# The first stage of a two-block transformer kernel rebuilt: own load buffers, sums and a bias table on TensorE, partial sums kept in banks

## The chip, the cores and the metric

The kernel runs on one core of one Trainium2 chip, with fp32 inputs and outputs for one sequence of 256 tokens. The metric is the device time of one execution in microseconds. Several runs are timed, and their median is what a prediction speaks of; one further execution was profiled.

## The reference

Two layers of a first block, then one layer of a second block, over x of 256 x 2048. Cut to what the change touches:

```
c_act = silu(c)
for l in range(2):
    mod = c_act @ w_mod[l] + b_mod[l]              # 2048 x 6144
    shift, scale, gate = split(mod, 3)
    h = rmsnorm(x, norm_gain[l]) * (1 + scale) + shift
    proj = h @ w_in[l]                             # q, k, v, gates, index heads
    ...
    bias = rel_bias[t5_bucket(pos[query] - pos[key])]   # 32 buckets, 8 heads
    logits = q @ k * scale + bias                  # sparse attention on the top 64 keys
    ...                                            # rotary, retention, group norm
    x = x + gate * (y @ w_out[l])
# second block: gated convolution, recurrence, a gate from the rmsnorm, final rmsnorm
```

t5_bucket gives a distance below 16 a bucket of its own and puts larger ones into 16 logarithmic buckets; distances of 128 and more share the last.

## The kernel before

Every product of the projections is made in three matmuls of split numbers. A weight chunk of 256 rows and up to 512 columns is loaded on SP's queue as `raw`; ACT rounds it to `whi` (L236), DVE subtracts to get `wlo` (L238), three buffers each. TensorE then does 12 matmuls per chunk (L254 hi by hi, L255 lo by hi, L256 hi by lo; two halves of the sequence, two row blocks), into two banks of the four that the tag `mm` has.

The input projection of layer 0 has ten column groups (nine of 512 columns, one of 336). Its rows of `w_in` are taken in four quarters, because the rows of h in quarter q need the modulation of just those 512 features. In each quarter all ten groups get two chunks, so 20 chunks or 240 matmuls a quarter. What a group has gathered is copied by ACT to a tile `sp` or `gate` in the first quarter (L931) and added there by DVE in the others (L934).

The modulation of a quarter (`mod_quarter`) loads 16 blocks of 512 KB (`graw`, in the first quarter `raw` too), which DVE multiplies by a scalar of c and adds up (L355, L357). Eight matmuls with one column each (L365) sum over partitions; L367 to L370 make shift `Sh` and gain `Gm`, and L560/L563 the rows of h from the transposed and normalised x. `first_rows` does all this as a background job. Its first part is the first stage: x is loaded on ACT's queue, vectors on POOL's (`vecs`, L304 and L312, transposed on TensorE in L315 and L316 and copied to `vT` by DVE), ACT squares x (L504), DVE reduces to `tot` (L534), POOL makes the reciprocal root in six small steps (`rstd`, L156 to L165), DVE makes two diagonal matrices `dg` (L540), and 32 matmuls (L203) transpose and scale x, which ACT copies back (L545).

The bias table is a background job from the second quarter on (`rel_rotary`, then `bias_table`): distances are computed on POOL and DVE and written to memory as bytes (`reld`), read back broadcast to 32 buckets by 4 rows (`rb`), turned to ones and zeros by three ACT passes (L483, L484, L486) in 24 blocks of 512, looked up with two matmuls a block (L469), copied (L471) and stored (`biasd`). Selection waits for it in the fourth quarter (`until("select")`).

A list scheduler with priorities (`tc.high_priority`, `AHEAD`) settles the order on each engine when the program is built; `spawn` gives a background job a rate at which its steps are mixed into the main work. Each engine then takes its instructions strictly in that order.

## Time and profile before

| what | us |
|---|---|
| median of three runs | 1931.42 (1928.2 to 1932.54) |
| the profiled execution, its own time | 1935.11 |
| its span, first to last instruction | 1933.3 |
| busy: PE, DVE, ACT, POOL | 1841.2, 1310.0, 1041.2, 109.0 |
| first main matmul starts at | 43.91 |
| the four quarters of layer 0's first projection end at | 101.39, 169.67, 236.19, 307.03 |

The ends of the quarters are read from the timeline of the main matmuls, 80 of L254 in each quarter. Since the program of each engine is a fixed queue, a stretch is best read by what TensorE does in it and what it waits for; the other engines' idle time matters only where TensorE waits for them.

### The profile page before, as it was taken

To read this page: it belongs to the slowest core of one execution; us is meant where nothing else is said; L and a number is where in the kernel's file an instruction comes from. 1 tells how busy PE (TensorE), PEld (TensorE's weight loads), DVE (VectorE), ACT (ScalarE), POOL (GpSimd) and SP (SyncE) were. 2 spreads that over 40 slices of the span, in tenths; PEclk is the share of its full clock that TensorE was granted. 3 is DMA by queue.
4 is the path that set the end of the run, shared out by engine and by line. 5 is a ranking of instruction groups with operands and counts; after the bars stand their busy time and mean duration, and the time that the engine had idled before them with its cause. 6 is when DMAs were issued, how large, how long until landed. Compare 5 with 4: busy or idle time off the path is not lost.

```text
span 1933.3 us, 24130 instructions
## 1 busy us (share of the span) xinstructions
PE 1841.2 (95%) x8670; PEld 1500.1 (78%) x8670; DVE 1310.0 (68%) x1705; ACT 1041.2 (54%) x1576; POOL 109.0 (6%) x220
## 2 busy tenths in 40 slices
PE   3989999998989999999999999999999999999997
PEld 3867677777867787788778778878887888888886
DVE  6788889988667779966655656656665545555564
ACT  3567674645445546356455764466545444445554
POOL 2000040002010005000110000000000000000100
PEclk9999999999989999999999999999999999999998
DMA  9988888887888999865557665556556666656664
GB/s 315 319 289 290 274 296 259 289 290 237 295 281 269 314 301 312 274 202 157 161 184 219 205 186 163 155 161 197 164 151 191 194 191 193 195 185 218 186 202 146
DMA packets 230921, 440.37 MB, mean 228 GB/s; under 512 B 19728, under 2 KB 32144, under 8 KB 230672
## 3 DMA queue, kind: packets, MB, share of 16 engines
q1 hardware_dynamic: 228880, 436.38, 71.3%
q10 hardware_dynamic: 1440, 2.34, 0.4%
q8 instruction: 68, 1.11, 0.2%
q14 instruction: 53, 0.43, 0.1%
q0 software_dynamic: 480, 0.10, 0.0%
HBM read 430.85 MB, written 7.91 MB: 227 GB/s over the span
## 4 chain that ended last, share of the span: by engine, by line
PE 64%; DMA 14%; DVE 10%; ACT 5%; issue 5%; POOL 2%; SPq 1%; ACTq 0%; DVEq 0%; POOLq 0%
PE mm L255 19%; PE mm L256 19%; PE mm L254 19%; DMA graw<-in_w_mod_dram 6%; DVE wlo L238 4%; DVE acc L357 2%; DMA rb<-reld 2%; DMA raw<-in_w_in_dram 2%; ACT whi L236 2%; PE tr L201 2%; DMA raw<-in_w_out_dram 1%; PE tr L1153 1%; DMA dec<-in_k_dec_dram 1%; DMA L<-biasd 1%; DMA raw<-in_w_mod_dram 1%
## 5 line engine op out<-in xcount | busy, mean ns | idle before, releaser
L238 DVE TENSOR_TENSOR wlo<-raw,whi 128x1024 fp32r<-128x1024 f32 (+1 forms) x596 | 721.0, 1212 | 408.8 <-ACT whi L236 407.0
L236 ACT CAST whi<-raw 128x1024 fp32r<-128x1024 f32 (+1 forms) x596 | 620.9, 1044 | 676.0 <-PE mm L256 437.2
L255 PE MATMUL mm<-wlo,ah 128*128 128x512 f32 (+1 forms) x2368 | 933.6, 394 | 14.1 <-DVE wlo L238 13.8
L254 PE MATMUL mm<-whi,ah 128*128 128x512 f32 (+1 forms) x2368 | 933.8, 397 | 13.7 <-ACT ah L192 7.8
L256 PE MATMUL mm<-whi,al 128*128 128x512 f32 (+1 forms) x2368 | 931.0, 393 | 0.5 <-DVE al L193 0.3
L255 PEld LDWEIGHTS mm<-wlo,ah 128*128 128x128 f32 x2368 | 447.5, 189 | 119.8 <-DVE wlo L238 32.6
L254 PEld LDWEIGHTS mm<-whi,ah 128*128 128x128 f32 x2368 | 446.4, 189 | 109.7 <-ACT whi L236 10.4
L256 PEld LDWEIGHTS mm<-whi,al 128*128 128x128 f32 x2368 | 447.1, 189 | 93.0 <-DVE al L193 2.4
L357 DVE SCALAR_TENSOR_TENSOR acc<-graw,ct,acc 128x1024 f32<-128x1024 f32 x174 | 222.7, 1280 | 51.5 <-DMA graw<-in_w_mod_dram 50.9
L934 DVE TENSOR_TENSOR sp<-sp,mm 128x512 f32<-128x512 f32 (+1 forms) x64 | 41.8, 657 | 8.4 <-PE mm L256 8.2
L201 PE MATMUL tr<-blob,ev 128*128 128x128 f32 x192 | 35.8, 277 | 11.5 <-DVE ev L1181 3.8
L184 ACT ACTIVATE ev<-tr,vT 128x128 f32<-128x128 f32 x112 | 32.4, 375 | 17.1 <-PE tr L201 17.1
L201 PEld LDWEIGHTS tr<-blob,ev 128*128 128x128 f32 x192 | 24.1, 141 | 21.2 <-issue 8.4
L156 POOL TENSOR_SCALAR rv<-tot 128x1 f32<-128x1 f32 (+1 forms) x9 | 2.8, 307 | 660.2 <-DVE tot L208 646.8
L504 ACT ACTIVATE junk<-xs 128x512 bf16<-128x512 f32 (+1 forms) x42 | 25.6, 610 | 22.1 <-DMA xs<-in_x_dram 10.0
L158 POOL TENSOR_TENSOR ry<-rv,mhalf 128x4 f32<-128x4 f32 (+2 forms) x33 | 31.8, 965 | 2.7
L201 PE MATMUL tr<-blob,xs 128*128 128x128 f32 x128 | 24.2, 281 | 5.3 <-ACT xs L995 3.6
L1153 PEld LDWEIGHTS tr<-X 128*128 128x128 f32 x224 | 27.0, 192 | 2.0 <-ACT uT L1203 1.0
L483 ACT ACTIVATE oh<-rb,blob 128x512 f32<-128x512 uint8 x24 | 16.4, 717 | 22.5 <-DMA rb<-reld 22.5
L1153 PE MATMUL tr<-X 128*128 128x128 f32 x224 | 27.5, 276 | 0.1
L156 POOL TENSOR_SCALAR rv<-ssq 128x4 f32<-128x4 f32 x12 | 4.5, 371 | 402.4 <-ACT junk L504 402.2
L156 POOL TENSOR_SCALAR rv<-var 128x4 f32<-128x4 f32 x8 | 5.2, 645 | 361.5 <-DVE var L853 361.3
(275 smaller groups left out, 1227.3 us busy)
## 6 DMA issues: line engine op xcount, KB each, us to landing
raw<-in_w_in_dram SPq DMA_DIRECT2D x416, 512.0 KB
graw<-in_w_mod_dram SPq DMA_DIRECT2D x186, 512.0 KB
raw<-in_w_out_dram SPq DMA_DIRECT2D x64, 512.0 KB
raw<-in_w_o_dram SPq DMA_DIRECT2D x32, 512.0 KB
raw<-in_w_ple_gate_dram SPq DMA_DIRECT2D x32, 512.0 KB
raw<-in_w_a_out_dram SPq DMA_DIRECT2D x16, 512.0 KB
raw<-in_w_b_out_dram SPq DMA_DIRECT2D x16, 512.0 KB
raw<-in_w_in_dram SPq DMA_DIRECT2D x16, 256.0 KB
```

Source lines behind the costliest of these rows:

```text
L158: G.tensor_tensor(y, v, mhalf[:, 0:n], op=OP.pow)
L184: A.activation(e[:, s], ps[:, s], AF.Copy, scale=gain[:, i:i + 1])
L201: T.transpose(ps[:, s], src[:, s], ident)
L236: A.copy(hi, raw)
L238: V.tensor_sub(lo, raw, hi.bitcast(F32))
L254: T.matmul(o, ah, hi[:, j, :], start=first, stop=False)
L255: T.matmul(o, ah, lo[:, j, :], start=False, stop=False)
L256: T.matmul(o, al, hi[:, j, :], start=False, stop=end)
L357: last[0] = V.scalar_tensor_tensor(acc, rf, ct[:, j:j + 1], acc, op0=OP.mult, op1=OP.add)
L504: A.activation(junk[:, :n], src, AF.Square, accum_out=acc)
L934: V.tensor_add(h, h, pt[:, :n])
L1153: T.matmul(ps[:, h * P:(h + 1) * P], X[:, h, s], X[:, h, s], start=True, stop=True)
```

## The change

**First quarter's modulation and rows.** They are written out in a function `first_quarter` that is called ahead of the layer. The first 13 of its 16 modulation blocks go to 256-KB tiles of their own (26 tiles `sw` in the tags `ah` and `al`); DVE sums them 512 wide. The last three blocks (`PEJ`) go to `graw` and are not added on DVE: TensorE sums them with the columns of `ct` as vector, 24 more matmuls of one column. The vector loads go from POOL's queue to ACT's; four of the eight x loads go to SP's. The copies to `vT`, the diagonals `dg` and half the copies of transposed x change between DVE and ACT.

**The bias table.** Positions, `rel_bias`, a constant `k_half` and the rows of distances are loaded on POOL's queue at the very start. Rows of distances (bf16, six tiles `rb` in the tags `whi` and `wlo`) are broadcast by a matmul with a selection matrix (L494), compared with the edges by one Sign activation (L496), looked up with two matmuls (L503), four blocks to a bank and one copy (L506). 11 of the 24 broadcasts use the `mm` banks. The table's 24 stores are the background job of the second quarter (`store_table`); the rest of its making, with the rotary tables, is in the first stage and the first quarter.

**Partial sums.** In the second and third quarter ACT copies a group's sums into its two banks before the group (L257), the matmuls add to them, and ACT copies the sums out (L999). Only the fourth quarter adds on DVE.

```diff
-AHEAD = {"wdma": 20, "whi": 30, "wlo": 35, "gdma": 0, "gdve": -10, "tail": -5}
-WJ, NB = 12, 6
+AHEAD = {"wdma": 20, "whi": 30, "wlo": 35, "gdma": 0, "gdve": -10, "tail": -5, "sums": 10}
 RAW, GRAW, WB, EV = 3, 3, 3, 5
+PEJ, EARLY = 3, 11
...
-        def wgroup(srcs, n, aT, kts, consumer, mode="k", tw=3):
+        def wgroup(srcs, n, aT, kts, consumer, mode="k", tw=3, sums=None):
 
             pts = [mmt(), mmt()]
+            if sums:
+                with tc.high_priority(offset=AHEAD["sums"]):
+                    for t in (0, 1):
+                        A.copy(pts[t][:, :n], sums[t][:, :n])
...
-                    first = ci == 0 and j == 0
+                    first = ci == 0 and j == 0 and not sums
...
-                G.dma_start(v1[r:r + n // P, 0:P], v[c0:c0 + n].rearrange("(r c) -> r c", c=P))
+                A.dma_start(v1[r:r + n // P, 0:P], v[c0:c0 + n].rearrange("(r c) -> r c", c=P))
...
-            V.tensor_copy(vT, ps[:, 0:P])
-            V.tensor_copy(vT2, ps[:, P:P + 64])
+            A.copy(vT, ps[:, 0:P])
+            A.copy(vT2, ps[:, P:P + 64])
...
+            rows = []
+            for n in range(6):
+                t, r0 = (0, 16 * n) if n < 2 else (1, 8 * n - 16)
+                rows.append(wp.tile([P, 2048], BF, name="rb", tag="wlo" if n % 2 else "whi", bufs=WB))
+                G.dma_start(rows[n][0:4], bass.AP(tensor=reld[t].tensor, offset=reld[t].offset + r0 * (t + 1) * P,
+                                                  ap=[[32 * (t + 1) * P, 4], [1, 2048]]))
+            for n in range(6):
+                t, r0 = (0, 16 * n) if n < 2 else (1, 8 * n - 16)
+                blocks = []
+                for i in range(4):
+                    bc = mmt() if 4 * n + i < EARLY else trt()
+                    T.matmul(bc, sel4[0:4], rows[n][0:4, i * 512:(i + 1) * 512], start=True, stop=True)
+                    sg = ap.tile([P, 512], F32R, name="sg", tag="qT", bufs=8)
+                    A.activation(sg, bc, AF.Sign, bias=edge)
+                    blocks.append(sg)
+                    if i < 3:
+                        yield
+                pm = mst()
+                for i, sg in enumerate(blocks):
+                    for k, pb in enumerate(parts):
+                        T.matmul(pm, pb[:, 96 - 32 * i:224 - 32 * i], sg, start=not i + k, stop=i + k == 4)
+                tag, bufs = ("L", 3) if n < 3 else ("gn", 2) if n < 5 else ("sc", 2)
+                bt = ap.tile([P, 512], F32, name="bt", tag=tag, bufs=bufs)
+                A.copy(bt, pm)
+                for i in range(4):
+                    stores.append((t, r0 + i * (512 // ((t + 1) * P)), bt[32 * i:32 * i + 32]))
+                yield
...
+        def first_quarter(ap):
             sq = sm(8, "sqx", 1)
             for kg in range(4):
                 for t in range(2):
                     xc[t][kg] = xs()
-                    A.dma_start(xc[t][kg], a["x"][0, t * P:(t + 1) * P, kg * 512:(kg + 1) * 512])
-            for kg in range(4):
+                    (Y if t else A).dma_start(xc[t][kg], a["x"][0, t * P:(t + 1) * P, kg * 512:(kg + 1) * 512])
+            posf, rel_b = distances(ap)
+            rot = rotary(ap, posf)
+            table = bias_table(ap, rel_b, stores)
+            acc = b1.tile([P, 1024], F32, name="acc", tag="acc", bufs=2)
+            pm = trt()
+            def sums(n, parts, vec):
+                for i in range(8):
+                    T.matmul(pm[:, 8 * n + i:8 * n + i + 1], parts[i // 4][:, i % 4 * P:i % 4 * P + P], vec,
+                             start=True, stop=True)
+            for j in range(16):
+                if j < 16 - GRAW:
+                    hw = [wp.tile([P, 512], F32, name="sw", tag=t, bufs=16) for t in ("ah", "al")]
+                    for o in range(2):
+                        last[1] = Y.dma_start(hw[o], wm[0][:, j, 2048 * o:2048 * o + 512])
+                else:
+                    raw = wp.tile([P, 2, 512], F32, name="graw", tag="graw", bufs=GRAW)
+                    src = wm[0][:, j, 0:512]
+                    last[1] = Y.dma_start(raw, bass.AP(tensor=src.tensor, offset=src.offset,
+                                                       ap=[list(src.ap[0]), [2048, 2], [1, 512]]))
+                    hw = [raw[:, 0, :], raw[:, 1, :]]
+                if j < 16 - PEJ:
+                    for o in range(2):
+                        ac = acc[:, 512 * o:512 * o + 512]
+                        if j == 0:
+                            V.tensor_scalar(ac, hw[o], ct[:, 0:1], None, op0=OP.mult)
+                        else:
+                            last[0] = V.scalar_tensor_tensor(ac, hw[o], ct[:, j:j + 1], ac, op0=OP.mult, op1=OP.add)
+                if j == 0:
+                    vec = vecs()
+                    next(vec)
+                    for kg in range(4):
+                        for t in range(2):
+                            square_sum(sq[:, 4 * t + kg:4 * t + kg + 1], xc[t][kg])
+                    next(table)
+                    with tc.high_priority(offset=60):
+                        tot = sm(2, "tot")
+                        V.tensor_reduce(tot, sq.rearrange("p (t k) -> p t k", t=2), axis=AX.X, op=OP.add)
+                        r = rstd(tot, 2, 1.0 / D)
+                if j in (3, 4):
+                    next(rot)
+                if j == 1:
+                    dgs = []
+                    for t in range(2):
+                        dg = wp.tile([P, P], F32, name="dg", tag="dg", bufs=2)
+                        A.activation(dg, ident, AF.Copy, scale=r[:, t:t + 1])
+                        dgs.append(dg)
+                    with tc.high_priority(offset=120):
+                        for kg in range(4):
+                            for t in range(2):
+                                ps = transpose4(xc[t][kg], dgs[t])
+                                if t:
+                                    A.copy(xc[t][kg], ps)
+                                else:
+                                    V.tensor_copy(xc[t][kg], ps)
+                if j > 1 and j % 4 != 2:
+                    for _ in zip(range(1), table):
+                        pass
+                if j == 13:
+                    for _ in vec:
+                        pass
+                if j == 16 - PEJ:
+                    sums(0, [acc[:, 0:512], acc[:, 512:1024]], ones[:, 0:1])
+                if j >= 16 - PEJ:
+                    sums(j - 15 + PEJ, hw, ct[:, j:j + 1])
+            s8 = sm(8, "sqx", 1)
...
+                    for i in range(4):
+                        A.activation(h[:, i, :], xc[t][0][:, i * P:(i + 1) * P], AF.Identity, scale=Gm[0][:, i:i + 1],
+                                     bias=Sh[0][:, i:i + 1])
+                    for i in range(4):
+                        p = slice(i * P, (i + 1) * P)
+                        V.tensor_scalar(h32[:, p], xc[t][0][:, p], Gm[0][:, i:i + 1], Sh[0][:, i:i + 1],
+                                        op0=OP.mult, op1=OP.add)
+                    V.tensor_sub(l.rearrange("p a b -> p (a b)"), h32, h.rearrange("p a b -> p (a b)").bitcast(F32))
+                    hT0[t][0] = h, l
...
-                    spawn(mark("select", rel_rotary(ap), bias_table(ap)), RATE["t5"])
+                    spawn(mark("select", store_table(stores)), RATE["t5"])
...
-                        if q == 0:
-                            if gi not in (3, 4):
+                        if q < per - 1:
+                            if q:
+                                pass
+                            elif gi not in (3, 4):
...
-                            if q == per - 1:
-                                return cons(t, held[gi, t], True)
-                    wgroup(srcs, n, hT, rows, spill, "first" if l and not q and not gi else "k")
+                            return cons(t, held[gi, t], True)
+                    wgroup(srcs, n, hT, rows, spill, "first" if l and not q and not gi else "k",
+                           sums=[held[gi, t] for t in (0, 1)] if 0 < q < per - 1 else None)
...
-        spawn(first_rows(), RATE["rows"])
...
+                if l == 0:
+                    rest = first_quarter(ap)
+                    es.enter_context(tc.issue_after(last[0].ins))
+                    es.enter_context(tc.issue_after(last[1].ins))
+                    spawn(first_rows(), RATE["rows"])
+                    spawn(rest, 0.5)
```

What this does to TensorE's queue shows from its start to the first main matmul. Before (L315, L316: vectors; L203: transposes; L365: modulation sums; L254: first main matmul):

```order
L315 MATMUL ms<-blob,ev 128x128
L316 MATMUL ms<-blob,ev 128x128
L203 MATMUL tr<-dg,xs 128x128 x32
L365 MATMUL tr<-blob,acc 128x1 x8
L254 MATMUL mm<-whi,ah 128x512
```

After, from the last lookups ahead of the transposes on (L211 is the line of the transposes now, L546 that of the modulation sums, L269 the first main matmul):

```order
L211 MATMUL tr<-dg,xs 128x128 x8
L503 MATMUL ms<-sg,rb 128x512
L211 MATMUL tr<-dg,xs 128x128 x8
L503 MATMUL ms<-sg,rb 128x512
L211 MATMUL tr<-dg,xs 128x128 x8
L503 MATMUL ms<-sg,rb 128x512 x2
L211 MATMUL tr<-dg,xs 128x128 x8
L546 MATMUL tr<-blob,acc 128x1 x8
L546 MATMUL tr<-ct,graw 128x1 x24
L503 MATMUL ms<-sg,rb 128x512 x2
L494 LDWEIGHTS sel_184
L494 MATMUL tr<-rb,sel_184 128x512
```

Ahead of these rows stand 11 broadcasts and 15 lookups; four lookups now stand between the transposes, three lookups and two broadcasts behind the sums, and the sums are 32 in place of 8.

On ACT the first stage reads before as follows (L504: squares; L545: copies of transposed x; L236: first weight cast; L560: rows of h):

```order
L525 DMA xs<-in_x_dram 128x512 x6
L504 ACTIVATE junk,sqx<-xs 128x512 x8
L545 COPY xs<-tr 128x512 x8
L236 CAST whi<-raw 128x1024
L560 ACTIVATE ev<-xs,Sh_79,Gm_77 128x128 x2
L236 CAST whi<-raw 128x1024
```

After, from the last vector loads to the diagonals (L522: squares; L333, L334: copies to `vT`; L496: Sign passes; L454 to L456: rotary; L506: table copy; L584: the diagonals):

```order
L327 DMA ev<-in_q_norm_gain_dram 2x128
L327 DMA ev<-in_k_norm_gain_dram 2x128
L522 ACTIVATE junk,sqx<-xs 128x512 x3
L333 COPY vT<-ms 128x128
L522 ACTIVATE junk,sqx<-xs 128x512
L334 COPY vT_75<-ms 128x64
L522 ACTIVATE junk,sqx<-xs 128x512 x3
L496 ACTIVATE sg<-mm,blob 128x512
L522 ACTIVATE junk,sqx<-xs 128x512
```

...and further:

```order
L496 ACTIVATE sg<-mm,blob 128x512
L456 ACTIVATE cs<-tmp,hp 128x64
L496 ACTIVATE sg<-mm,blob 128x512 x3
L506 COPY bt<-ms 128x512
L496 ACTIVATE sg<-mm,blob 128x512 x2
L584 ACTIVATE dg<-blob,rz 128x128 x2
L496 ACTIVATE sg<-mm,blob 128x512 x3
```

The squares now stand behind 11 loads and, the last five, behind the copy to `vT`; the diagonals are now ACT's and stand behind eight Sign passes.

In the second quarter the partial sums change engines. Before, on DVE (L934: additions; L238: wlo; L357: modulation blocks):

```order
L934 TENSOR_TENSOR gate<-gate,mm 128x512 x2
L238 TENSOR_TENSOR wlo<-raw,whi 128x1024 x2
L357 SCALAR_TENSOR_TENSOR acc<-graw,ct,acc 128x1024
L238 TENSOR_TENSOR wlo<-raw,whi 128x1024
L357 SCALAR_TENSOR_TENSOR acc<-graw,ct,acc 128x1024
L934 TENSOR_TENSOR gate<-gate,mm 128x512 x2
L357 SCALAR_TENSOR_TENSOR acc<-graw,ct,acc 128x1024
L238 TENSOR_TENSOR wlo<-raw,whi 128x1024
```

After, on ACT (L244: whi; L257: copies into banks; L999: copies out):

```order
L244 CAST whi<-raw 128x1024
L257 COPY mm<-sp 128x512
L999 COPY sp<-mm 128x512
L244 CAST whi<-raw 128x1024
L999 COPY sp<-mm 128x512
L257 COPY mm<-sp 128x512 x2
L244 CAST whi<-raw 128x1024
L999 COPY sp<-mm 128x512
```

DVE has no addition in that quarter now, and ACT has two copies in and two out for each group between its casts.

## Rows read from the trace of the kernel before

**Rows 1.** The page: the span, engines' busy time, and costly groups, with mean ns.

```profile
span 1933.3 us, 24130 instructions
...
PE 1841.2 (95%) x8670; PEld 1500.1 (78%) x8670; DVE 1310.0 (68%) x1705; ACT 1041.2 (54%) x1576; POOL 109.0 (6%) x220
...
L238 DVE TENSOR_TENSOR wlo<-raw,whi 128x1024 fp32r<-128x1024 f32 (+1 forms) x596 | 721.0, 1212 | 408.8 <-ACT whi L236 407.0
L236 ACT CAST whi<-raw 128x1024 fp32r<-128x1024 f32 (+1 forms) x596 | 620.9, 1044 | 676.0 <-PE mm L256 437.2
...
L934 DVE TENSOR_TENSOR sp<-sp,mm 128x512 f32<-128x512 f32 (+1 forms) x64 | 41.8, 657 | 8.4 <-PE mm L256 8.2
...
L483 ACT ACTIVATE oh<-rb,blob 128x512 f32<-128x512 uint8 x24 | 16.4, 717 | 22.5 <-DMA rb<-reld 22.5
```

**Rows 2.** Windows, one a quarter: length, busy time by engine, clock, DMA share, GB/s.

```profile
43.90:101.39 57.49, 57.48 (x257) 47.67 (x257) 44.14 (x47) 32.77 (x47) 0.00 (x0) 0.95 0.95 323
101.39:169.67 68.28, 61.65 (x274) 46.68 (x272) 56.21 (x79) 45.76 (x72) 2.61 (x2) 1.00 0.87 285
169.67:236.19 66.52, 62.94 (x280) 47.31 (x278) 55.62 (x62) 48.15 (x74) 0.00 (x0) 1.00 0.88 288
236.19:307.03 70.84, 69.46 (x351) 53.80 (x350) 61.82 (x115) 50.86 (x107) 20.96 (x36) 1.00 0.82 268
```

**Rows 3.** Windows, tile mm alone: one weight chunk of 512 columns, mid first quarter.

```profile
66.60:69.31 2.71, 2.71 (x13) 2.25 (x12) 0.00 (x0) 0.59 (x1) 1.00 1.03 370
```

**Rows 4.** Waits of PE, 100 to 165 us: total, times, longest.

```profile
PE mm L255 <- DVE wlo L238: 3.4, 3, 1.8
PE mm L254 <- ACT whi L236: 3.1, 3, 1.3
```

**Rows 5.** Windows, line L469 alone (the lookups), second to fourth quarter.

```profile
101.39:169.67 68.28, 5.13 (x16) 1.57 (x16) 1.00 0.87 285
169.67:236.19 66.52, 7.61 (x22) 2.06 (x22) 1.00 0.88 288
236.19:307.03 70.84, 3.12 (x10) 0.97 (x10) 1.00 0.82 268
```

**Rows 6.** Timeline of the first stage: start, length, engine, line, idle before.

```profile
4.73 8.09 ACTq L525 DMA_DIRECT2D xs<-in_x_dram  x5
...
9.47 0.50 POOL L312 DMA_DIRECT2D ev<-in_k_norm_gain_dram  x1
...
13.62 0.63 ACT L504 ACTIVATE junk<-xs 128x512 bf16<-128x512 f32 x1
...
14.88 0.45 PE L316 MATMUL ms<-blob,ev 128*128 128x128 f32 x1 [4.05 <-DMA ev<-in_k_norm_gain_dram]
...
23.14 0.15 DVE L534 TENSOR_REDUCE tot<-sqx 128x2 f32<-128x8 f32 x1
...
26.34 0.19 POOL L165 TENSOR_TENSOR rz<-ry,rq 128x2 f32<-128x2 f32 x1
...
37.04 0.59 ACT L545 COPY xs<-tr 128x512 f32<-128x512 f32 x1 [0.36 <-PE tr L203]
...
40.35 0.16 DVE L370 SCALAR_TENSOR_TENSOR Gm<-mq,vT 128x4 f32<-128x4 f32 x1
...
42.02 0.60 DVE L563 TENSOR_SCALAR ev<-xs,Gm,Sh 128x128 f32<-128x128 f32 x2
...
43.91 0.79 PE L254 MATMUL mm<-whi,ah 128*128 128x512 f32 x1 [3.86 <-ACT ah L192]
```

**Rows 7.** Windows, line L203 alone (the first transposes), in two halves.

```profile
26.90:31.98 5.08, 5.07 (x23) 5.07 (x24) 1.00 0.56 193
32.32:36.78 4.46, 4.46 (x41) 4.44 (x39) 1.00 0.80 262
```

**Rows 8.** Windows, line L365 alone (eight modulation sums), by granted clock.

```profile
37.72:39.06 1.34, 1.33 (x13) 1.34 (x13) 1.00 1.05 393
39.06:40.05 0.99, 0.99 (x6) 0.91 (x5) 0.50 1.07 393
```

190 lines of the change are left out of this document (71 added, 119 removed).

## The prediction

> **What bounds the kernel now.** I read the page first [rows 1]: TensorE is busy 95% of the span of 1933.3 us (the profiled execution's own time is 1935.1, the median of the runs shown 1931.4), so the change can pay only where TensorE stands idle or works on something it could be spared. The table by stretch [rows 2] shows where. Between 43.9 and 307 us lie the four quarters of the first input projection. The first is busy 57.48 of 57.49 us. The second and third are 68.28 and 66.52 us long and idle for 6.6 and 3.6 us. The first matmul of the projection stands at 43.91 us [rows 6]; all before it is preparation. One weight chunk of 12 matmuls takes 2.71 us when nothing interferes [rows 3], .227 us a matmul; 240 of them, 24 of these narrower, make 52.8 us: that is the floor of a quarter.
>
> What lies between floor and length in the second quarter? The waits [rows 4] name whi and wlo, the split weights made by ACT and DVE: 6.5 us. The 16 lookups of the bias table cost 5.1, 22 in the third quarter cost 7.6, 10 in the fourth 3.1 [rows 5]. On ACT each block of that table takes three passes of .72 and a copy (.59, by the nearest row) that stand between the casts; on DVE 20 additions of partial sums of .66 us (13 us a quarter) stand between the subtractions [rows 1].
>
> **First stage, step by step** (before: [rows 6]). The vector loads leave POOL's queue for ACT's, behind four x loads; there ACT was busy issuing until 12.8 us with eight. I put the last of the 11 at 15 us, between 12.8 and 17. The k_norm load was issued at 9.47 and used at 14.88, so a trip of 4.9 us: vectors on TensorE at 19.9, copied on ACT at about 21. This copy now stands in ACT's queue ahead of the last squares, which before waited for nothing but x. Four squares (.63 and .19 each, 3.3) and a Sign pass (.72, priced as a pass of the old table) follow: the total that was reduced at 23.14 us comes at about 25. The rstd chain on POOL took 3.4 us; two loads of table rows now stand inside it, about .5 each as the k_norm issue: 29.4. The diagonals, on DVE before, stand on ACT behind seven Sign passes (5.0), a table copy (.6) and three small rotary steps (an estimate of .8, between one and two such passes), so about 31.4 against 26.9. If the rows arrive late, all this moves with them.
>
> The 32 transposes: before, the first 23 records took 5.07 us and the next 41 took 4.46 [rows 7], so .89 to 1.7 us for a tile of 8 records. TensorE will just have done 26 table matmuls (by the change's order), so I take .89 for each of eight tiles, and .23 for four lookups between them: 39.4 us, where before it was 36.8. Then 32 sums instead of 8, since three modulation blocks are added on TensorE; this spares the last block's 1.28 us additions on DVE but not TensorE's time: 13 records took 1.33 us at granted clock 1.00, 6 took .99 at .50 [rows 8]: .205 and .33 a matmul of two records, 6.6 to 10.6 us; I take 8: 47.4. DVE then needs .45 as before; eight tensor_scalars (.30, 2.4 in all) stand in its queue ahead of the first wlo (1.21). Five more table matmuls behind the sums (1.2) are hidden by this. The first wlo matmul comes at 51.5, where before the first hi matmul ended at 44.7 [rows 6]: **+6.8 us**. From both sides: with diagonals at 26.9 and sums at .205 it is +1; with everything at half clock +15.
>
> **First quarter.** 30 table matmuls stay in it (10 broadcasts, 20 lookups) at .23, 6.9 us; by the lookups' own mean of .32 it would be 9.6. The table's row tiles occupy whi and wlo buffers, two of three at times, so a cast waits for the chunk two back, where before it waited for three back: chunk time 2.71 against cast 1.04 and subtraction 1.21 leaves .46 for handovers. I put 1.5 (bounds 0 and 7). Its 57.5 becomes 65.9: **+8.4**.
>
> **Second and third.** Lookups go from 16 to 6 with one broadcast (7 matmuls), then from 22 to 0. The partial sums leave DVE: its 56.2 us of work in the second quarter becomes about 43. They go to ACT as 40 copies, half of them into the banks ahead of the group, half out behind it, at .59 [rows 6]: 23.6. ACT loses eight blocks of (3 x .72 + .59), 22.0 us: 45.8 becomes about 47 of some 57. TensorE: floor 52.8, modulation sums 1.7, table 1.6, remaining stalls 1.5 make 57.6 against 68.3, **-10.7**; third 52.8 + 1.7 + 1.5 = 56.0 against 66.5, **-10.5**. The stalls may also stay at 6.6 and 3.6, or vanish. DMA could forbid this: the first quarter moved 323 GB/s for 57.5 us at a share of .95, 18.6 MB; the third would need 332 GB/s. The first quarter shows that a quarter of 57.5 is fed without a wait for weights, so this bound costs at most 1.5 in the third.
>
> The preload is a new wait: a group's first matmul waits for ACT's copies into its two banks, which wait for the consumer of the group two back. Behind them in ACT's queue stand casts, and behind these everything. Four banks hold two groups, so a copy has a group's 5.4 us; it costs nothing so long as ACT is not full.
>
> **Fourth quarter.** 10 lookups less (2.3) and their ACT passes (.7 of stalls): **-3.0**. The additions stay there. The 24 stores of the finished table move on SP's queue into the second quarter, where the row reads and stores of the old table stood; I cost them at nothing.
>
> **Sum:** 6.8 + 8.4 - 10.7 - 10.5 - 3.0 = -9.0, so 1926.1 against the profiled 1935.1 and **1922 against the median**. I call 0.2% (3.9 us) the least that can be told from no change: faster lies below 1927.6, slower above 1935.3.
>
> **Rivals.**
> **B, the short start.** If small loads land in about half of those 4.9 us, the vectors are there when the squares are done, the rows' three trips in series (positions, distances out, rows back) are over before the diagonals are asked for, and the start is only 1 us later: 1922 - 5.8 = 1916. For it: on ACT's queue nothing measured contradicts it, since the vector loads of before were POOL's. Against it: 4.9 us in the one row that I have. The Trainium skill ("DMA: Bandwidth & Descriptors", Anatomy of one DMA — SWDGE (gpsimd) path) gives some 2.0 us fixed per DMA on POOL's path; by that rule the vectors land at 17 and B follows, but the 4.9 us of the row, on that same path, disagree with it. Chance 0.22.
> **C, the half-speed start, on the slower side.** TensorE's table work follows ACT's Sign passes (.72 for three matmuls of .23), with gaps. If it runs at half speed through table, transposes and sums: eight tiles at 1.70 and four lookups at .45 cost 7.4 more, sums at .33 2.6 more, and the 26 early table matmuls end about 4 us later: +14, 1936. It becomes slower than before when the start is more than 13 us worse than forecast in A. For it: the granted clock stood at .50 behind the gap ahead of the sums [rows 8], and the first 23 transpose records are twice as long. Against it: much of the table work overlaps the wait for rstd anyway. Chance 0.11.
> **D, ACT as the new bound.** The stalls of second and third quarter do not shrink but grow, because casts stand behind copies that wait for TensorE. If each of 18 group changes costs .7 us, 12.6: 1934.6. For it: 40 copies a quarter on an engine that is in order, and a copy out that waits for the group's last matmul with the casts behind it. Against it: 47 of 57 us busy, and the first quarter of before had 20 such copies out with no stall. Chance 0.12.
> **E, two buffers are too few.** If handovers take .35 over the .46 for each of the 20 chunks, the first quarter loses 7 instead of 1.5: 1928. For it: cast, subtraction and matmul then stand in one loop. Against it: the casts run ahead when the buffers come back, which is in the course of the first quarter. Chance 0.12.
>
> **How the numbers follow.** A (as summed) 0.43, its own range 1914 to 1932; B 0.22, C 0.11, D 0.12, E 0.12. Likeliest 1922. The range runs to 1909 (B with stalls that vanish) and to 1936 (C, D). Faster: A .34, B .22, C .00, D .01, E .03, together .60. Same: A .08, C .03, D .06, E .08, together .25. Slower: A .01, C .08, D .05, E .01, together .15.
>
> **What would show it.** The first main matmul pair followed by a gap to 51.5 us; the vT copy on ACT near 21 and tot near 25; first quarter near 66 us, second near 57.6, third near 56, with DVE below 45 us busy in them and waits on whi and wlo below 2 us. If tot comes by 23, B. If the 32 sums take over 10 us, C. If TensorE waits for L257's copies or for whi more than 6 us a quarter, D. If TensorE waits for whi in the first quarter in nearly every chunk, E. The forecast is wrong altogether if the fourth quarter or what follows it gets longer by what the earlier ones gain, for instance since the loads run ahead no further.

## The result, and the profile after

The changed kernel takes 1966.7 us (1962.6 to 1969.2, four runs) against 1932.0 for the kernel before in the same session: ratio 1.0173, 95% interval 1.0154 to 1.0191. It is 35 us slower where 10 less were forecast, outside the range. The profiled execution took 1965.4 us, 30.3 more than the one profiled before.

The page after, its span and busy time (to be set beside [rows 1]), and the table by stretch, now with the first stage as a row of its own and the boundaries at the first main matmul of each quarter ([rows 2] are the old quarters):

```profile
span 1963.6 us, 24241 instructions
...
PE 1869.4 (95%) x8744; PEld 1521.6 (77%) x8744; DVE 1289.9 (66%) x1685; ACT 1043.6 (53%) x1592; POOL 108.0 (6%) x217
```

```profile
0.00:65.49 65.49, 38.43 (x168) 26.64 (x168) 27.61 (x77) 22.30 (x52) 12.33 (x25) 0.94 0.65 211
65.49:133.82 68.33, 67.14 (x287) 51.46 (x287) 47.78 (x46) 42.61 (x64) 0.00 (x0) 0.96 0.88 293
133.82:199.54 65.72, 61.42 (x265) 47.38 (x263) 43.19 (x42) 47.43 (x79) 0.00 (x0) 0.97 0.82 272
199.54:264.02 64.48, 58.12 (x257) 45.20 (x256) 43.98 (x43) 43.56 (x70) 0.00 (x0) 1.00 0.90 296
264.02:331.32 67.30, 65.62 (x341) 52.51 (x340) 61.11 (x112) 38.76 (x85) 20.38 (x36) 1.00 0.85 282
```

The same first-stage row of the kernel before, not shown so far:

```profile
0.00:43.91 43.91, 13.26 (x82) 12.49 (x83) 24.71 (x34) 16.19 (x33) 11.02 (x26) 0.94 0.89 308
```

Set side by side: the first main matmul is 21.6 us later (forecast 6.8). The first quarter takes 68.3 in place of 57.5 (+10.8, forecast +8.4), the second 65.7 in place of 68.3 (-2.6, forecast -10.7), the third 64.5 in place of 66.5 (-2.0, forecast -10.5), the fourth 67.3 in place of 70.8 (-3.5, forecast -3.0). That makes 24.3 us at the end of the fourth quarter; the other 6.0 of the profiled 30.3 come behind it. The relief itself came: DVE is busy 43.2 and 44.0 us in the second and third quarter, as forecast. TensorE did not get faster for it. The DMA share, the last column but one, is what moved: .65 in the first stage where it was .89.

How the first stage became late is read from its timeline (start, length, engine, line; the counterparts are in [rows 6] and [rows 7]):

```profile
17.12 0.49 DVE L434 TENSOR_SCALAR tmp<-tmp 128x256 bf16<-128x256 int32 x2
...
18.76 0.27 ACTq L327 DMA_DIRECT2D ev<-in_k_norm_gain_dram  x1
19.07 0.63 ACT L522 ACTIVATE junk<-xs 128x512 bf16<-128x512 f32 x1 [14.95 <-DMA ev<-in_hg_norm_g_dram]
...
28.48 1.86 PE L494 MATMUL mm<-rb,sel 4*128 4x512 bf16 x4 [6.25 <-DMA rb<-reld]
...
29.10 0.69 ACT L496 ACTIVATE sg<-mm,blob 128x512 fp32r<-128x512 f32 x1 [3.68 <-PE mm L494]
...
30.43 0.16 DVE L576 TENSOR_REDUCE tot<-sqx 128x2 f32<-128x8 f32 x1 [2.96 <-ACT junk L522]
...
35.53 0.72 POOL L173 TENSOR_TENSOR rz<-ry,rq 128x2 f32<-128x2 f32 x1
...
38.22 0.70 ACT L584 ACTIVATE dg<-blob,rz 128x128 f32<-128x128 f32 x2
...
42.67 3.62 PE L211 MATMUL tr<-dg,xs 128*128 128x128 f32 x16
...
52.80 1.95 PE L546 MATMUL tr<-blob,acc 128*128 128x1 f32 x16
...
62.74 0.19 DVE L605 TENSOR_REDUCE sqx<-tr 128x8 f32<-128x32 f32 x1 [9.99 <-PE tr L546]
...
65.49 0.80 PE L269 MATMUL mm<-whi,ah 128*128 128x512 f32 x1
```

The vector loads stand on ACT ahead of the squares, so the first square starts at 19.07 (before, squares ran at 13.62). The distances' clamp on DVE (L434), whose input POOL had ready by about 11.5 us, starts at 17.12: it stood behind a modulation step that waited for its block. So the table's rows land only at 28.48. The last square stands behind a Sign pass that waits for them, and `tot` comes at 30.43, not 25. rstd (the reciprocal root) ends at 36.25, the diagonals start at 38.22 behind more Sign passes, and the first transposes at 42.67 behind 26 table matmuls. These ran slowly. Windows of the lookups alone, and of the sums alone:

```profile
28.00:43.00 15.00, 9.35 (x15) 3.79 (x15) 1.00 0.96 342
```

```profile
52.80:54.60 1.80, 1.80 (x16) 1.80 (x17) 1.00 0.00 0
54.60:62.70 8.10, 8.10 (x50) 8.01 (x49) 0.66 0.43 129
```

15 lookups are on TensorE for 9.35 us though the clock column reads 1.00; all 26 table matmuls from 28.4 to 42.6 us keep it busy for 14.1, .54 each. The column misleads here. The first clock record of this trace begins at 46.89 us, and the column reads 1.00 where there is no record. A broadcast and two lookups of the changed kernel, and the same three in run e3 (below), where the clock was on record at .50, take the same 1.68 us (the fourth that is counted is the end of the matmul before):

```profile
31.43:33.11 1.68, 1.68 (x4) 1.00 1.01 360
```

```profile
55.07:56.75 1.68, 1.68 (x4) 0.50 0.79 274
```

The transposes show it too: 16 records take 3.27 us ahead of 46.89 and 1.69 behind it.

```profile
42.67:45.94 3.27, 3.27 (x16) 3.27 (x15) 1.00 0.07 24
48.71:50.40 1.69, 1.68 (x16) 1.69 (x16) 1.00 0.00 0
```

So TensorE ran at the lower of its two levels (1.2 GHz) through the 26 table matmuls and the first transposes. The halves of [rows 7] part in the same way: the kernel before has its first clock record at 32.2 us, where its transposes become twice as fast.

The 32 sums take 1.8 us for the first eight and 8.1 for the rest, at a granted clock of .66 on average: 9.9 in all, where I took 8.

While this went on, DMA stood still. Waits of SP's queue from 44 to 66 us, and the busy share of DMA in 40 slices of 1.5 us, 40 to 100 us:

```profile
SPq L363 <- PE tr L546: 20.2, 2, 17.9
```

```profile
DMA  9410000000028470005960695899999799999959
GB/s 399 158 37 5 0 0 0 11 0 0 0 23 307 100 269 0 0 0 78 363 258 0 120 328 175 237 364 295 294 355 341 152 370 410 380 358 396 351 127 307
```

The same 60 us around the first main matmul of the kernel before, 24 to 84 us:

```profile
DMA  9991467999994899992799798899999999999999
GB/s 389 388 356 51 105 244 131 401 404 397 385 370 49 284 391 385 345 340 90 176 374 384 193 363 274 310 388 300 388 359 392 382 325 347 399 365 352 384 281 311
```

SP's queue waits up to 17.9 us with the next modulation load, because the last three blocks of the first quarter hold the three `graw` buffers until TensorE has summed them, and the weight loads stand behind it in the queue. (The weight buffers were full too, as e14 shows.) Before, DMA was rarely below half in that stretch.

### The profile page after: what moved, and what is told of

Same layout as the page of the kernel before. It is cut to its first block, busy times and chain, and to the rows that moved or that the text cites. A ratio compares the mean times of both kernels' runs of the same rounds, so it can differ in the third digit from the quotient of the medians.

```text
span 1963.6 us, 24241 instructions
## 1 busy us (share of the span) xinstructions
PE 1869.4 (95%) x8744; PEld 1521.6 (77%) x8744; DVE 1289.9 (66%) x1685; ACT 1043.6 (53%) x1592; POOL 108.0 (6%) x217
## 3 DMA queue, kind: packets, MB, share of 16 engines
q1 hardware_dynamic: 227376, 435.68, 70.5%
## 4 chain that ended last, share of the span: by engine, by line
PE 68%; DMA 11%; DVE 10%; ACT 4%; issue 4%; POOL 2%; SPq 0%; DVEq 0%; ACTq 0%; POOLq 0%
PE mm L270 20%; PE mm L271 20%; PE mm L269 20%; DMA graw<-in_w_mod_dram 6%; DVE wlo L246 4%; PE tr L209 2%; ACT whi L244 1%; PE tr L1226 1%; DVE acc L369 1%; DMA raw<-in_w_out_dram 1%; DMA raw<-in_w_in_dram 1%; PE ms L503 1%; DVE I L737 1%; POOL ry L166 1%; DMA ev<-in_b_mod_dram 1%
## 5 line engine op out<-in xcount | busy, mean ns | idle before, releaser
L244 ACT CAST whi<-raw 128x1024 fp32r<-128x1024 f32 (+1 forms) x596 | 621.6, 1044 | 677.3 <-PE mm L271 490.3
L269 PE MATMUL mm<-whi,ah 128*128 128x512 f32 (+1 forms) x2368 | 937.5, 398 | 8.2 <-ACT whi L244 4.5
L269 PEld LDWEIGHTS mm<-whi,ah 128*128 128x128 f32 x2368 | 448.2, 190 | 105.4 <-ACT whi L244 9.1
L369 DVE SCALAR_TENSOR_TENSOR acc<-graw,ct,acc 128x1024 f32<-128x1024 f32 x165 | 211.1, 1279 | 50.5 <-DMA graw<-in_w_mod_dram 50.0
L999 ACT COPY sp<-mm 128x512 f32<-128x512 f32 (+1 forms) x64 | 35.8, 565 | 27.6 <-PE mm L271 27.6
L522 ACT ACTIVATE junk<-xs 128x512 bf16<-128x512 f32 (+1 forms) x42 | 25.6, 609 | 25.5 <-DMA ev<-in_hg_norm_g_dram 14.9
L166 POOL TENSOR_TENSOR ry<-rv,mhalf 128x4 f32<-128x4 f32 (+2 forms) x33 | 35.8, 1084 | 2.7
L209 PEld LDWEIGHTS tr<-blob,xs 128*128 128x128 f32 x128 | 16.8, 146 | 13.2 <-ACT xs L1062 7.3
```

What stands on the lines that cost most here:

```text
L166: G.tensor_tensor(y, v, mhalf[:, 0:n], op=OP.pow)
L209: T.transpose(ps[:, s], src[:, s], ident)
L244: A.copy(hi, raw)
L269: T.matmul(o, ah, hi[:, j, :], start=first, stop=False, skip_group_check=skip)
L369: last[0] = V.scalar_tensor_tensor(acc, rf, ct[:, j:j + 1], acc, op0=OP.mult, op1=OP.add)
L522: A.activation(junk[:, :n], src, AF.Square, accum_out=acc)
```

## The experiments

All ran in one layout: profile, and timed runs beside the kernel before on the same chip. "Idle" is worked out from the table by stretch of each run: length times (1 - DMA share), summed from the start to the end of the third quarter; as the shares are rounded to .01, it is good to about 1 us.

| run | median us (before) | ratio (95%) | first main | quarters 1, 2, 3 | end of 3 | idle |
|---|---|---|---|---|---|---|
| before | 1932.0 | | 43.9 | 57.5, 68.3, 66.5 | 236.2 | 24.6 |
| changed | 1966.7 (1932.0) | 1.0173 (1.0154-1.0191) | 65.5 | 68.3, 65.7, 64.5 | 264.0 | 49.4 |
| e1 | 1964.2 (1935.3) | 1.0159 (1.0134-1.0185) | 62.6 | 67.5, 65.4, 66.6 | 262.0 | 49.8 |
| e2 | 1943.9 (1935.3) | 1.0040 (1.0018-1.0062) | 43.8 | 56.9, 71.1, 73.5 | 245.3 | 33.0 |
| e4 | 1958.5 (1935.3) | 1.0115 (1.0093-1.0138) | 59.6 | 66.8, 65.4, 66.1 | 257.9 | 44.0 |
| e5 | 1957.9 (1935.3) | 1.0120 (1.0083-1.0157) | 54.0 | 60.4, 69.2, 72.3 | 255.8 | 42.9 |
| e3 | 1962.2 (1932.3) | 1.0153 (1.0116-1.0189) | 71.9 | 67.6, 61.5, 66.1 | 267.0 | 52.3 |
| e6 | 1953.0 (1932.3) | 1.0110 (1.0078-1.0142) | 62.0 | 68.5, 65.9, 66.0 | 262.5 | 53.1 |
| e6c | 1956.6 (1932.3) | 1.0124 (1.0101-1.0146) | 64.1 | 68.7, 66.8, 66.1 | 265.7 | 52.7 |
| e7 | 1943.9 (1932.3) | 1.0057 (1.0029-1.0085) | 64.9 | 69.2, 58.4, 56.3 | 248.8 | 53.2 |
| e10 | 1944.2 (1932.7) | 1.0064 (1.0043-1.0085) | 43.7 | 56.9, 69.8, 69.3 | 239.6 | 28.6 |
| e11 | 1956.6 (1932.7) | 1.0129 (1.0107-1.0151) | 53.3 | 76.6, 60.3, 67.3 | 257.4 | 28.7 |
| e12 | 1936.9 (1932.7) | 1.0024 (1.0006-1.0043) | 43.2 | 56.3, 67.4, 67.0 | 233.8 | 24.3 |
| e13 | 1967.7 (1932.7) | 1.0192 (1.0164-1.0220) | 62.6 | 82.9, 67.5, 54.6 | 267.5 | 32.7 |
| e14 | 1956.8 (1933.1) | 1.0119 (1.0099-1.0139) | 58.8 | 65.4, 65.6, 64.5 | 254.3 | 42.8 |
| e15 | 1952.3 (1933.1) | 1.0101 (1.0081-1.0122) | 48.6 | 60.0, 70.5, 71.7 | 250.9 | 38.4 |

**e1: partial sums back on DVE.**
```diff
-                        if q < per - 1:
+                        if q == 0:
-                           sums=[held[gi, t] for t in (0, 1)] if 0 < q < per - 1 else None)
```


> The changed kernel with one part undone: DVE adds the partial sums in the second and third quarter again, ACT copies nothing into the banks. The first stage and the table stay. Theory 1 (casts stand in ACT's queue behind copies out that wait for the group's last matmul, so whi comes late): the second and third quarter shrink from 65.7 and 64.5 us to about 60 and 58, in all about 1955 us. Rival 1 (the stalls are from the late start or from weights that DMA brings late): both quarters stay within 1.5 us, about 1966 us.


Second and third quarter are 65.4 and 66.6: my theory of that moment, casts stuck behind copies out, falls as the bound. The waits say why the length stays. In these two quarters of the changed kernel, the copies out wait for TensorE, and SP's queue waits for a weight buffer that wlo frees, but the casts hardly wait for a weight:

```profile
ACT sp L999 <- PE mm L271: 21.9, 16, 3.0
ACT whi L244 <- DMA raw<-in_w_in_dram: 2.5, 4, 1.5
SPq L239 <- DVE wlo L246: 69.9, 34, 4.9
```

In e1, without the copies, the casts wait for weights instead:

```profile
ACT whi L244 <- DMA raw<-in_w_in_dram: 45.9, 22, 4.2
```

It does not matter for the time which engine adds the sums here.

**e2: the sums on ACT alone, in the kernel before.** The lines of `wgroup`, `spill` and the call as in the change.


> The kernel before with one part alone: partial sums of the second and third quarter are copied into the banks and out by ACT, nothing else changes. Theory 1: ACT has 24 us more in each of these quarters beside the table's passes, 69 us of work in a stretch of 67, so each grows by 5 us or more and the whole comes to about 1945. Rival 2 (the copies cost nothing and DVE's 13 us a quarter were what held the weights): both quarters shrink by 3 us or more, about 1925.


+2.9 and +7.0 us in the two quarters, 1944: on an ACT that also makes the old table, the copies cost. In the change they replace that work and cost nothing visible.

**e4: no blocks on TensorE.**
```diff
-PEJ, EARLY = 3, 11
+PEJ, EARLY = 0, 11
+            if PEJ == 0:
+                sums(0, [acc[:, 0:512], acc[:, 512:1024]], ones[:, 0:1])
```


> The changed kernel with all 16 modulation blocks of the first quarter added on DVE, so that TensorE makes 8 sums in place of 32. Theory 2 (the 32 one-column sums cost 9.9 us on the path, against 2.3 for 8): they take 2.3 to 2.7, DVE's six added steps of .74 lie partly in its wait, first main matmul at about 61 in place of 65.5, about 1961 to 1962 in all. Rival (DVE's added steps take the place of the sums): first main matmul at 65 or later, 1966.


First main matmul at 59.6, 1958.5: the 24 added sums and the hold on `graw` cost 2 to 6 us of start (kernels with the same first stage start from 62.0 to 65.5).

**e5: the first stage alone.** Table, rotary tables and partial sums as in the kernel before; own buffers, vector loads on ACT, 32 sums as in the change.


> The kernel before with the rebuilt loads, the inline first quarter and the 32 sums alone: the bias table and the rotary tables are a background job of the second to fourth quarter again, in their old form, and DVE adds the partial sums. Theory 3 (of the 21.6 us by which the first main matmul is late, about 9 belong to vector loads ahead of the squares and to the 32 sums, and 12 to the table's blocks): tot at about 26 us, first main matmul at 52 to 54, quarters as in the kernel before, about 1941. Rival (the table only fills time that is idle anyway): first main matmul at 60 or later, about 1950.


The first main matmul came at 54.0 as expected, but the quarters did not stay as before: 12.4 us more over the four, though their work is the old one; 1958. Timeline of e5:

```profile
18.19 0.63 ACT L518 ACTIVATE junk<-xs 128x512 bf16<-128x512 f32 x1 [14.07 <-DMA sw<-in_w_mod_dram]
...
25.99 0.15 DVE L568 TENSOR_REDUCE tot<-sqx 128x2 f32<-128x8 f32 x1
...
29.47 0.20 POOL L175 TENSOR_TENSOR rz<-ry,rq 128x2 f32<-128x2 f32 x1
...
30.16 10.14 PE L213 MATMUL tr<-dg,xs 128*128 128x128 f32 x64 [9.81 <-ACT dg L574]
...
41.99 7.20 PE L539 MATMUL tr<-ct,graw 128*128 128x1 f32 x48
...
54.02 1.22 PE L271 MATMUL mm<-whi,ah 128*128 128x512 f32 x2 [4.83 <-ACT whi L246]
```

`tot` is 2.9 us later than in [rows 6], for the vector loads alone (first square at 18.19); the transposes start 3.3 later and take as long as before; the sums end at 49.2 where they ended at 40.06. e1 differs from e5 in the bias table and the rotary tables alone and starts 8.5 us later: that is their price. The rest of the changed kernel's 21.6 is spread between kernels with the same first stage (first main matmul from 62.0 to 65.5 in the changed kernel, e1, e6, e6c, e7 and e13).

**e3: the table held behind the transposes.**
```diff
+                    with tc.issue_after(tr_mm[-1].ins), tc.issue_after(dg_ins.ins):
                         for _ in zip(range(1), table):
                             pass
```


> The changed kernel with the table's blocks held back: the Sign passes stand behind the diagonals on ACT, the table's matmuls behind the 32 transposes on TensorE; same work. Theory 4 (the rows of distances come late, and what stands behind them in the queues of ACT and TensorE is late with them, 12 us in all): tot at about 26 us in place of 30.4, first transposes at about 32 in place of 42.7; the table's matmuls then lie on the path ahead of the first main matmul, some 35 at .25 to .4, so that of the 10.7 us 0 to 4 are left at the first main matmul. Rival (the start is late for the transposes and sums themselves): first transposes at 40 or later.


`tot` at 25.48 and first transposes at 30.29, as expected: the table's blocks ahead of them, with their late rows, were what held both. But the main matmuls started at 71.9, later than in the changed kernel and outside what I expected: the transposes' copies on DVE now waited among modulation steps, and the table's matmuls ran on the path, in the middle of the sums, at half speed. Moved, the work is no cheaper.

**e6 and e6c: four raw buffers, and the control.**
```diff
-RAW, GRAW, WB, EV = 3, 3, 3, 5
+RAW, GRAW, WB, EV = 4, 3, 3, 4
```


> The changed kernel with four raw weight buffers in place of three (and, for the space, four ev tiles in place of five). Theory 5 (second and third quarter are held by the loop of a raw buffer: load of 5 to 6 us, cast, subtraction, and both of the last stand behind copies in their queues; three buffers are out for 8.2 us at full speed): TensorE's waits in these quarters, 8.4 and 9.7 us by start-to-start times, halve, each quarter 4 us shorter, about 1957. Rival 5a (the load rate itself is the bound): no change in the quarters. Rival 5b (the order of casts and copies out at a group's end is what costs): no change either, waits once a group as before.

> The control for the run with four raw buffers: four ev tiles in place of five alone. All theories: within 2 us of the changed kernel, 1965.


Waits of PE over the second and third quarter, of the changed kernel and of e6:

```profile
PE mm L270 <- DVE wlo L246: 6.6, 11, 1.1
PE mm L269 <- ACT whi L244: 3.5, 6, 1.4
```

```profile
PE mm L270 <- DVE wlo L246: 7.3, 13, 1.1
PE mm L269 <- ACT whi L244: 3.3, 5, 1.4
```

No less. Theory 5 falls: a fourth raw buffer is not it. (In e6 SP's queue waits 47.6 us for raw buffers and 31.2 for the modulation's, which stayed at three.) The control came out 8 us under what was expected of it, all of it behind the fourth quarter; why is not shown.

**e7: half the modulation loads.** Every second block is used twice from the second quarter on; DVE's work is unchanged, 4.2 MB a quarter are not loaded.
```diff
+                again = l == 0 and ranges[0] < 2048 and j % 2
+                if not again:
                     raw = wp.tile([P, 2, 512], F32, name="graw", tag="graw", bufs=GRAW)
```


> The changed kernel, with the modulation of the second to fourth quarter's rows loading only every second block (each block loaded is used twice, so DVE's work is the same and 4.2 MB a quarter are not moved; the modulation is then another one). Rival 5a (load rate): second and third quarter 5 us shorter or more. Theory 5 (a buffer's loop): 2 to 4 us shorter, by loads that land earlier. Rival 5b (the order at a group's end): unchanged to within 1.5 us.


Windows of e7, second and third quarter:

```profile
134.08:192.51 58.43, 58.16 (x265) 47.97 (x263) 42.06 (x40) 45.89 (x74) 0.00 (x0) 0.98 0.78 254
192.51:248.76 56.25, 55.62 (x257) 45.77 (x256) 42.97 (x42) 45.64 (x73) 0.00 (x0) 1.00 0.91 309
```

58.4 and 56.3 us, idle on TensorE .3 and .6: with 8 of 36 loads a quarter gone, the forecast's 57.6 and 56.0 appear, with all copies of partial sums still on ACT. The step that failed was the one on transfers. The run takes bytes and places in SP's queue away together, so it does not tell the rate of transfers from their order.

**e10: the kernel before without the table's work on chip.** Loads and stores stay; the ACT passes, lookups and copies are gone.
```diff
-                    A.activation(oh, oh, AF.Relu, bias=bhw)
-                    A.activation(ohr, oh, AF.Relu, bias=ones[:, 0:1], scale=-1.0)
...
-                    T.matmul(pm[0:32, :], pb, ohr, start=n == 0, stop=n == 1)
```


> The kernel before without the table's work on chip: its loads and stores stay, its three ACT passes, its two lookups and its copy a block are left out (so the bias is zero). Theory 6 (second and third quarter are bound by the 36 loads of 512 KB that each needs, so relief of ACT and TensorE is worth little there): second and third quarter shorter by at most 3 us each, about 1927. Rival, the step as the prediction put it (floor, modulation sums and 1.5 us of stalls): 57 to 59 us each, about 1912.


Windows of e10, second and third quarter:

```profile
100.56:170.34 69.78, 61.11 (x257) 47.44 (x256) 57.71 (x81) 27.34 (x40) 2.19 (x2) 0.95 0.84 274
170.34:239.59 69.25, 60.07 (x258) 46.16 (x256) 54.49 (x61) 23.73 (x29) 0.00 (x0) 0.98 0.86 275
```

ACT is busy 27 and 24 us where it was 46 and 48 [rows 2], TensorE has 16 and 22 matmuls less, and the quarters are not shorter: 69.8 and 69.3. What ACT was spared became a wait for weights. Casts' waits over the two quarters, of the kernel before and of e10:

```profile
ACT whi L236 <- DMA raw<-in_w_in_dram: 8.4, 8, 3.2
```

```profile
ACT whi L236 <- DMA raw<-in_w_in_dram: 60.5, 27, 5.6
```

The table's share of the prediction's two largest terms is refuted in the kernel before itself; DVE's additions stayed in this run. That the quarters grew by 1.5 and 2.7 is not explained.

**e11 and e13: modulation loads on POOL's queue,** in the kernel before and in the changed one.
```diff
+                    q = G if l == 0 and 0 < c0 < 2048 else Y
+                    last[1] = q.dma_start(dst, src)
```


> The kernel before with the modulation loads of the second to fourth quarter's rows on POOL's queue in place of SP's, where they stand among the weight loads and wait with them. Theory 6 with its second half (DMA stands idle at the quarters' changes because a modulation load stands behind a weight load that waits for a buffer): the idle stretches are filled, second and third quarter 3 to 6 us shorter each, about 1922. Rival (the loads collide more, a weight load then lands later): no shorter or longer, 1932 to 1940.

> The changed kernel with the modulation loads of the second to fourth quarter's rows on POOL's queue. Theory 6 with its second half: the stretch of idle DMA ahead of the first main matmul stays (the modulation's buffers are held until the 32 sums), the ones at the quarters' changes are filled: first quarter as it is, second and third 3 to 6 us shorter each, about 1957. Rival (collisions): 1966 or more.


The rival held in its direction; e11 went well past its 1940. Freed from SP's order, the modulation loads run ahead: 77.7 and 80.6 MB have been moved by the end of the third quarter, against 70.7 before. The first quarter grows to 76.6 and 82.9 us (and in e11 the first main matmul moves to 53.3), later ones shrink (60.3; 54.6). The loss moves, the sum does not shrink.

**e12: the kernel before with four ev tiles.**


> The kernel before with four ev tiles in place of five. The changed kernel came out 10 us shorter with four; if that is from the later stages' order and not from its first stage, the same here: about 1925. If not, 1932.


1936.9, slightly slower: nothing to gain, and the control's 8 us belong to the changed kernel alone.

**e14 and e15: own buffers for all 16 blocks,** in the changed kernel (8 sums on TensorE), and alone in the kernel before with vector loads on POOL's queue.
```diff
-                if j < 16 - GRAW:
+                if True:
```


> The changed kernel with all 16 modulation blocks of the first quarter in tiles of their own and added on DVE (8 sums), so that the three graw tiles are free for the second quarter's blocks from the start. Theory 7 (in all kernels so far 70.7 to 71 MB are moved by the end of the third quarter, which ends after 212 to 215 us of transfers plus the time that DMA idles, and the change idles 25 us more, 18 of them ahead of the first main matmul): the idle time falls by the three loads and what follows them, at least 5 us under that of the run without TensorE's blocks (44.0), and the third quarter ends at 250 to 254 in place of 257.9. Rival (it is the late first main matmul itself that is carried on, not the transfers): third quarter ends as late after the first main matmul as there, 198 us.

> The kernel before with the inline first quarter and all its 16 modulation blocks in tiles of their own, added on DVE with 8 sums; vector loads on POOL's queue, table and partial sums as before. Theory 7: first main matmul at 43 to 46, idle time of DMA to the end of the third quarter at 20 to 25 us, third quarter ends at 233 to 238, about 1928 to 1934 in all; the version that could beat both. Rival (13 or 16 loads in flight at the start delay x and the vectors, so the diagonals come late): first main matmul at 48 or later, 1938.


e14's idle time fell by only 1.2 us against e4, and the third quarter ended 195.5 us after the first main matmul, not 198.3: theory 7's size for it was wrong, since the three raw buffers, full and waiting for the first wlo (one wait of SP's queue is 11.5 us), stop the loads just as well. In e15 the end of the third quarter is 202.3 us behind the first main matmul where the kernel before has 192.3, with 13.8 us more idle: a late first matmul alone does not explain the lag. Idle transfers go with it; what makes them idle is not shown. Timeline of e15:

```profile
9.10 0.63 ACT L518 ACTIVATE junk<-xs 128x512 bf16<-128x512 f32 x1 [4.97 <-DMA xs<-in_x_dram]
...
18.97 0.16 DVE L568 TENSOR_REDUCE tot<-sqx 128x2 f32<-128x8 f32 x1 [0.74 <-ACT junk L518]
...
21.13 0.70 POOL L170 TENSOR_TENSOR rq<-ry 128x2 f32<-128x2 f32 x1
...
22.59 0.19 POOL L172 TENSOR_SCALAR rq<-rq 128x2 f32<-128x2 f32 x1
...
23.55 9.44 PE L213 MATMUL tr<-dg,xs 128*128 128x128 f32 x64 [8.55 <-DMA sw<-in_w_mod_dram]
...
40.25 3.54 PE L539 MATMUL tr<-blob,acc 128*128 128x1 f32 x16 [7.26 <-DVE acc L559]
...
48.60 1.22 PE L271 MATMUL mm<-whi,ah 128*128 128x512 f32 x2 [4.80 <-ACT whi L246]
```

With vector loads off ACT's queue and x split over two, `tot` comes at 18.97, 4.2 us earlier than in [rows 6], and the transposes at 23.55. But 32 half-width modulation steps on DVE reach to 40.25 where 16 full ones ended at 37.6, and the first casts stand behind the rows of h. No version here beats the kernel before.

## Why the prediction was wrong

**What held for all runs that load the same.** By the end of the third quarter 70.3 to 71.6 MB have been moved in the kernel before, the changed one and e1 to e6c, e10, e12, e14 and e15 (length times GB/s, summed). Where the end of the third quarter lies follows: idle time plus 209 to 215 us of transfers, in each of them (before 236.2 - 24.6 = 211.6; changed 264.0 - 49.4 = 214.6; e15 250.9 - 38.4 = 212.5). The other three fit by their bytes: e7 moves 64.1 MB in 196 us, e11 and e13 77.7 and 80.6 MB in 229 and 235. This is bookkeeping, and idle time can be the effect of a late kernel as well as its cause; it tells what an edit must come to if it is to pay: DMA idles less or moves less. The change lets it idle 24.8 us more, 18 of them ahead of the first main matmul, and its third quarter ends 27.8 later.

**First stage, forecast +6.8, measured +21.6.** The clause "If the rows arrive late, all this moves with them" was the right worry and had no term in the sum: that is the step that failed here, together with the full clock that the sum gave to TensorE. By step: `tot` 30.43 for 25 (a Sign pass waiting for rows ahead of the last square; e3 without it: 25.48); rstd and its loads 5.8 for 4.4; the diagonals 2.0 behind that, as forecast; then 4.5 us of table matmuls ahead of the transposes, at .54 a matmul and not .23. "TensorE will just have done 26 table matmuls, so I take .89" for a tile was wrong in its reason: those matmuls, 14.1 us of them, did not bring the clock up; it rose at 46.89, 4.2 us into the transposes. The first two tiles took 3.6 us (16 records from 42.67), the others about 1 each; with four lookups 10.1 us, not 8.0. The sums took 9.9, not 8. Rival C, half speed, had this mechanism, and it accounts for some 8.5 of the 14.8 us by which the start missed the forecast (4.5, 2.1 and 1.9); the rest, to within .5, is late rows (5.4 in `tot`) and rstd (1.4). That C's own 14 comes so near the whole is luck; it was given 0.11. Rival B is out: the k_norm load, issued on ACT's queue by 19.03, was used at 21.79, 2.8 us later where the row of before has 4.9, so B's premise nearly held; but it was issued 3.8 us later than I had put the last load, and the rows' three trips ended only at 28.48. The last of them, on POOL's path, took 6.2 us. The Trainium skill ("DMA: Bandwidth & Descriptors", Anatomy of one DMA — SWDGE (gpsimd) path) gives a fixed cost of some 2.0 us on that path; this trip took three times that, and no run here shows what the rest was.

**First quarter, +8.4 against +10.8.** Right within its bounds; its 31 table matmuls took 9.3 us, near the 9.6 by the lookups' own mean and not 6.9. Rival E is out: TensorE waits for whi or wlo only .5 us in it.

**Second and third quarter, -21.2 against -4.6.** The failed step is "The first quarter shows that a quarter of 57.5 is fed without a wait for weights, so this bound costs at most 1.5 in the third." One quarter that started with its loads ahead was taken as a rate for all. e7 shows that with 8 of 36 loads gone the forecast's own numbers appear; e10 that the table's relief alone is worth nothing, since the casts then wait 60.5 us for weights; e1 and e6 that neither the engine of the sums nor a fourth raw buffer matters. The waits on whi and wlo [rows 4] were read as ACT and DVE having too much work; relief of that work only uncovers the wait for weights. Rival D, ACT as the bound, is half there: the copies out do wait for TensorE in the changed kernel (21.9 us for `sp` alone), with casts behind them. But e1, without copies, is no shorter, and e7, with all of them, is as short as forecast, so they are not the bound; in the old kernel e2 shows that they cost. Why DMA still idles for 10 to 18% of these quarters is not settled. SP's queue stands 69.9 us waiting for weight buffers, yet a fourth one (e6) and another queue for the modulation (e11, e13) are not the answer alone.

**Fourth quarter, -3.0 against -3.5.** Right.

**The rest, forecast 0, measured +6.0 in the profile** (4.4 more by the medians). From the end of the fourth quarter on, the runs' profiles differ among themselves: 1606.2 us from there to TensorE's last instruction in e6, 1613.6 before, 1619.6 in the changed kernel, 1624.0 in e10. The cause stays open.

**The preload of banks** did what was forecast: no wait of TensorE names L257.

## What to carry to other kernels

Before pricing relief on an engine, add up bytes to the end of the stretch and the idle time of DMA: here all variants that moved the same bytes gained nothing from relief elsewhere. Work put into an idle start is free only if its inputs are there early: here three loads in series made it late, and in-order queues passed the lateness to all that stood behind it. Price it at the speed that TensorE has there, too: .54 us a matmul here, not .23. A load buffer that is handed to another engine at the end of a stage holds up not only its own next load but the whole queue of loads behind it; what that costs depends on the other buffers, which here were full as well (e14).

## What the runs showed of the hardware

- POOL's small steps of rstd take .19 us when DVE is idle and .6 to .7 while it works through modulation steps: the last of them takes .19 before [rows 6] and .72 in the changed kernel (L173); in e15, L170 at 21.13 takes .70 and L172 at 22.59, after DVE's row of steps, .19. Those steps lengthened rstd. The Trainium skill ("GPSIMD Engine Reference", Specifications) says that POOL shares its SBUF interfaces with VectorE and contends with VectorE's instructions that have two SBUF inputs; the modulation steps have two, and the trace agrees.
- The granted clock fell during the one-column sums: after 1.8 us of them at 1.00 it averages .66 over the next 8.1, and .52 over the first 5.5 us of main matmuls behind them (65.5 to 71.0). Whether the sums or the 128-column transposes ahead of them brought it down is not shown.
- The 26 table matmuls kept TensorE busy for 14.1 of 14.2 us and ran at half clock from end to end. The clock column read 1.00 throughout, for the trace has no clock record there; the time from one matmul to the next (.53 to .59 us, as in e3 at .50) tells it.
